# A gated linear unit on one core: the stores move from the ScalarE queue to the sync queue, behind the loads

## The chip, the core and the metric

The kernel runs on one core of one Trainium2 chip. The metric is the device time of one execution in microseconds (us). A difference of about 0.2% is what the measurement of this kernel can tell from no change.

## What is computed

The input `x` is 8192 x 8192 in float32. Its left half is `a`, its right half is `b`, and the result is 8192 x 4096:

```python
def reference(x):
    a, b = np.split(x, 2, axis=-1)
    return a * (1 / (1 + np.exp(-b)))
```

So 268.4 MB are read and 134.2 MB are written, and each output element needs one sigmoid and one product.

## The kernel before

**Tiles.** The rows are cut into 32 tiles of 256 rows. A tile has 128 partitions with two whole rows each, so a load is 128 x 16384 elements (64 KB in a partition, 8.39 MB in all) and a store is 128 x 8192 elements (32 KB in a partition, 4.19 MB). There are two slots (`SLOTS = 2`): two input tiles `x_sb0` and `x_sb1`, and two output tiles `o_sb0` and `o_sb1`. Tile i uses slot i modulo 2 of both.

**Work on a tile** (`work`, from L53). ScalarE takes the sigmoid of the `b` half in place (L61), and VectorE multiplies the `a` half by it into the output tile (L72). A middle tile is one piece: one activation and one product of 128 x 8192. The first and the last tile are cut into four pieces of 128 x 2048.

**Loads** (`load`, L46 to L51). All are issued on the sync queue, SP. Load i + 2 goes into the slot of tile i, so it waits until the products have counted up to the last one of tile i (`self.done[i]`, L50). Loads 0 and 1 wait for nothing; load 0 is moved ahead of the program's body.

**Stores** (`store`, L78 to L89). The store of a middle tile is issued on the ScalarE queue, ACT (L81, L82), and waits for the same count as load i + 2, the last product of tile i (L83). The last tile's store is cut into four pieces of 1 MB, one for each piece of the work, and these are issued on SP. When a store has landed it adds 16 to the slot's semaphore `ready` (L88). The first activation on a slot adds 1 to the same semaphore (L66), and the product waits for both together (L64, L65, L73): a product on tile i starts when its sigmoid is done and when store i - 2, which read the same output slot, has landed.

**Order** (`trace`, L91 to L104). It is written out by hand: load 1; then for each i the work of tile i, load i + 2 (if there is one) and store i (if i is not the last); then the four stores of the last tile. Each engine's sequencer goes through its own instructions in this order, and an instruction that waits holds up those behind it on the same engine. Before the change SP thus holds load 1, load 2, load 3 and so on and the four last stores, and ACT holds the activations of tile 0, store 0, the activation of tile 1, store 1 and so on. The data itself is moved by 16 DMA engines that serve both queues; q1 is the row of SP's transfers in the profile, q10 that of ACT's.

**End** (`close`). Each engine's drain, a wait for the last whole store, a clearing of the semaphores, and SP's wait for the four last stores (L118).

Of the kernel before, what the change touches and what calls it, by code (L numbers as in the profile page):

```python
# [1 line left out]

# [4 lines left out]

P = 128
R = 2
SLOTS = 2  # L10


class _Program:

    def __init__(self, nc, x, out):
        self.nc = nc
        fp32 = mybir.dt.float32
        n_rows, n_cols = x.shape
        self.half = n_cols // 2  # L30
        self.n_tiles = n_rows // (P * R)
        self.x = x.rearrange("(n p r) m -> n p (r m)", p=P, r=R)
        self.out = out.rearrange("(n p r) m -> n p (r m)", p=P, r=R)
        self.xs = [nc.alloc_sbuf_tensor(f"x_sb{s}", [P, R * n_cols], fp32).ap() for s in range(SLOTS)]
        self.os = [nc.alloc_sbuf_tensor(f"o_sb{s}", [P, R * self.half], fp32).ap() for s in range(SLOTS)]
        self.loaded = [nc.alloc_semaphore(f"loaded{s}") for s in range(SLOTS)]
        self.ready = [nc.alloc_semaphore(f"ready{s}") for s in range(SLOTS)]
        self.product = nc.alloc_semaphore("product")
        self.sigmoid = nc.alloc_semaphore("sigmoid")
        self.arrived = nc.alloc_semaphore("arrived")  # L40
        self.last = nc.alloc_semaphore("last")
        self.to_ready = [0] * SLOTS
        self.products = self.sigmoids = self.lasts = 0
        self.done = {}

    def load(self, i, after=None):  # L46
        s = i % SLOTS
        ins = self.nc.sync.dma_start(out=self.xs[s][:, :], in_=self.x[i]).then_inc(self.loaded[s], 16)
        if i >= SLOTS:
            ins._wait_ge(self.product, self.done[i - SLOTS])  # L50
        return ins  # L51

    def work(self, i, pieces):  # L53

        nc, s = self.nc, i % SLOTS
        rows = self.xs[s].rearrange("p (r h m) -> p r h m", r=R, h=2)
        packed = self.os[s].rearrange("p (r m) -> p r m", r=R)
        waits = []
        for k, (r, c) in enumerate(pieces):
            b = rows[:, r, 1, c]  # L60
            sig = nc.scalar.activation(out=b, in_=b, func=mybir.ActivationFunctionType.Sigmoid)  # L61
            if k == 0:
                sig._wait_ge(self.loaded[s], 16 * (i // SLOTS + 1))
                self.to_ready[s] += 1 + (16 if i >= SLOTS else 0)  # L64
                waits.append((self.ready[s], self.to_ready[s]))  # L65
                sig.then_inc(self.ready[s], 1)  # L66
            else:
                self.sigmoids += 1
                waits.append((self.sigmoid, self.sigmoids))
                sig.then_inc(self.sigmoid, 1)  # L70
        for (r, c), wait in zip(pieces, waits):
            mul = nc.vector.tensor_mul(out=packed[:, r, c], in0=rows[:, r, 0, c], in1=rows[:, r, 1, c])  # L72
            mul._wait_ge(*wait)  # L73
            mul.then_inc(self.product, 1)
            self.products += 1
        self.done[i] = self.products

    def store(self, i, lo=0, hi=None, products=None):  # L78
        s, final = i % SLOTS, i == self.n_tiles - 1
        hi = R * self.half if hi is None else hi  # L80
        queue = self.nc.sync if final else self.nc.scalar  # L81
        ins = queue.dma_start(out=self.out[i][:, lo:hi], in_=self.os[s][:, lo:hi])  # L82
        ins._wait_ge(self.product, self.done[i] if products is None else products)  # L83
        if final:
            self.lasts += 16
            ins.then_inc(self.last, 16)
        else:
            ins.then_inc(self.ready[s], 16)  # L88
        return ins  # L89

    def trace(self):  # L91

        n, half = self.n_tiles, self.half
        whole = [(slice(0, R), slice(0, half))]
        fourths = [(slice(r, r + 1), slice(h * half // 2, (h + 1) * half // 2)) for r in range(R) for h in range(2)]
        self.load(1)
        for i in range(n):
            self.work(i, fourths if i in (0, n - 1) else whole)
            if i + SLOTS < n:
                self.load(i + SLOTS)  # L100
            if i < n - 1:
                self.store(i)
        for k in range(4):
            self.store(n - 1, k * half // 2, (k + 1) * half // 2, self.products - 3 + k)  # L104

    def close(self):


        nc, s = self.nc, (self.n_tiles - 2) % SLOTS
        for engine in (nc.scalar, nc.vector, nc.sync):  # L110
            engine.drain().then_inc(self.arrived, 1)  # L111
        nc.gpsimd.wait_ge(self.arrived, 3)
        nc.gpsimd.wait_ge(self.ready[s], self.to_ready[s] + 16)
        ids = sorted(h.num for h in (*self.loaded, *self.ready, self.product, self.sigmoid, self.arrived))
        assert ids == list(range(ids[0], ids[-1] + 1)) and self.last.num not in ids
        nc.gpsimd.sem_clear(range(ids[0], ids[-1] + 1))
        nc.gpsimd.drain()
        nc.sync.wait_ge(self.last, self.lasts).then_inc(self.last, -self.lasts)  # L118


def _launch_early(nc):

    SP = mybir.EngineType.SP
    entry, body = (b.instructions for b in nc.main_func.blocks[:2])
    load = next(i for i in body if i.engine == SP and i.opcode == "DMACopy")
    assert not load.sync_info.on_wait
    body.remove(load)
    where = next(k for k, i in enumerate(entry) if i.engine == SP and i.opcode == "Drain")  # L130
    entry.insert(where, load)


@with_exitstack
def kernel(
    ctx: ExitStack,
    tc: tile.TileContext,
    x: bass.AP,
    out: bass.AP,
):  # L140
    nc = tc.nc
    prog = _Program(nc, x, out)
    tc.info.no_tile_sem_insts.add(prog.load(0).ins.name)
    tc.close()
    tc.compile()  # L145
    _launch_early(nc)
    prog.trace()
    prog.close()


# [1 line left out]
_INS = ['x']  # L152
_OUTS = [((8192, 4096), 'float32')]


# [23 lines left out]
```

## Time and profile before

| | |
|---|---|
| median of 3 runs | 933.18 us (933.16 to 934.11) |
| the profiled execution | 933.08 us |
| its span, from the first to the last instruction | 931.8 us |
| VectorE busy | 278.6 us (30% of the span), 38 products |
| ScalarE busy | 226.8 us (24%), 38 activations and a table load |
| moved by DMA | 402.67 MB, mean 432 GB/s over the span |
| one activation of 128 x 8192 | 7.03 us |
| one product of 128 x 8192 | 8.69 us |
| one activation, one product of 128 x 2048 | 1.90 us, 2.29 us |
| issue of a load on SP, of a store on ACT (median) | 0.33 us, 0.36 us |

The profile is of one execution, and its times run from the start of its span. "DMA share" in a stretch of time is the mean busy share of the 16 DMA engines, and GB/s is what they moved; both count a packet whole at its start, so a short stretch can show a share over 1. A "landing" is the moment at which all 16 parts of a transfer have reported to its semaphore. "Issue to landing" starts when the sequencer issues the transfer, so it holds the time that the transfer stands in its queue.

### The profile page before, as it was taken

Reading aid. Unit: us, or ns where it says so; the run is one execution under the profiler, and the core shown is the slowest. Engines: PE = TensorE matmul, PEld = TensorE weight load, DVE = VectorE, ACT = ScalarE, POOL = GpSimd, SP = SyncE. Lnnn points to the kernel's source line nnn. Section 1 sums busy time; section 2 is a strip of 40 time slices with the busy share of each in tenths; the row PEclk is TensorE's granted clock in tenths of the full one; section 3 lists DMA queues with packets and bytes.
Section 4 is the critical chain, followed back from the end, with each engine's and each line's share of the span. In section 5 each row is a group of like instructions: output and inputs, shape, how many; then the busy total and the mean of one; then the engine's idle time right before and its main releaser. Section 6 shows DMA issues by size and latency. Waiting matters only on the chain.

```text
span 931.8 us, 190 instructions
## 1 busy us (share of the span) xinstructions
DVE 278.6 (30%) x38; ACT 226.8 (24%) x39; POOL 0.2 (0%) x4
## 2 busy tenths in 40 slices
DVE  0333213333133331233312333123331233312333
ACT  1323330233311333113331133311333203332033
POOL 0000000000000000000000000000000000000000
DMA  9999999999999999999999999999999999999999
GB/s 405 428 450 428 422 456 405 450 428 428 450 421 435 428 436 442 428 428 450 450 405 430 442 456 428 412 463 408 450 428 428 450 408 447 428 428 450 426 429 405
DMA packets 9649, 402.67 MB, mean 432 GB/s; under 512 B 1072, under 2 KB 1072, under 8 KB 1072
## 3 DMA queue, kind: packets, MB, share of 16 engines
q1 hardware_dynamic: 5184, 272.63, 67.7%
q10 hardware_dynamic: 4464, 130.03, 32.3%
q14 instruction: 1, 0.01, 0.0%
HBM read 268.44 MB, written 134.22 MB: 432 GB/s over the span
## 4 chain that ended last, share of the span: by engine, by line
DMA 73%; DVE 15%; ACT 12%; DVEq 0%; issue 0%
DMA x_sb<-in_x_dram 73%; DVE o_sb L72 15%; ACT x_sb L61 12%; DVEq L111 0%
## 5 line engine op out<-in xcount | busy, mean ns | idle before, releaser
L72 DVE TENSOR_TENSOR o_sb<-x_sb 128x8192 f32<-128x8192 f32 (+1 forms) x38 | 278.6, 7344 | 647.1 <-ACT x_sb L61 647.1
L61 ACT ACTIVATE x_sb<-x_sb 128x8192 f32<-128x8192 f32 (+1 forms) x38 | 225.5, 5949 | 693.9 <-DMA x_sb<-in_x_dram 693.9
L61 ACT ACT_TABLE_LOAD x1 | 1.3, 1283 | 1.4 <-PEq L145 1.4
L163 POOL MEMSET const-bfloat16-1.0<- 128x1 bf16 x1 | 0.1, 102 | 0.0
L163 POOL MEMSET const-uint8-127<- 128x1 uint8 x1 | 0.1, 102 | 0.0
L163 POOL MEMSET const-float32-0.0<- 128x1 f32 x1 | 0.1, 99 | 0.2 <-issue 0.2
L163 POOL MEMSET const-float32-1.0<- 128x1 f32 x1 | 0.1, 99 | 0.0
## 6 DMA issues: line engine op xcount, KB each, us to landing
out_dram<-o_sb ACTq DMA_DIRECT2D x31, 4096.0 KB, 34.8
out_dram<-o_sb SPq DMA_DIRECT2D x4, 1024.0 KB, 5.7
x_sb<-in_x_dram SPq DMA_DIRECT2D x32, 42.2
```

The lines of the kernel that those rows point to most:

```text
L61: sig = nc.scalar.activation(out=b, in_=b, func=mybir.ActivationFunctionType.Sigmoid)
L72: mul = nc.vector.tensor_mul(out=packed[:, r, c], in0=rows[:, r, 0, c], in1=rows[:, r, 1, c])
L163: nc = _bacc.Bacc("TRN2", target_bir_lowering=False, num_devices=1)
```

## The change

The store's queue is no longer chosen: every store is issued on SP. Load i + 2 and store i keep their waits, both for the last product of tile i, and the written order is the same, so that SP now holds load 1, load 2, store 0, load 3, store 1, up to load 31, store 29, store 30 and the four last stores. Tiles, slots, pieces and semaphores stay as they are.

```diff
     def store(self, i, lo=0, hi=None, products=None):
         s, final = i % SLOTS, i == self.n_tiles - 1
         hi = R * self.half if hi is None else hi
-        queue = self.nc.sync if final else self.nc.scalar
-        ins = queue.dma_start(out=self.out[i][:, lo:hi], in_=self.os[s][:, lo:hi])
+        ins = self.nc.sync.dma_start(out=self.out[i][:, lo:hi], in_=self.os[s][:, lo:hi])
         ins._wait_ge(self.product, self.done[i] if products is None else products)
```

## The prediction

> **What bounds the kernel now.** I read the page first: the row of the DMA engines, the queues, and the chain that ended last.
>
> ```profile
> DMA  9999999999999999999999999999999999999999
> ...
> q1 hardware_dynamic: 5184, 272.63, 67.7%
> q10 hardware_dynamic: 4464, 130.03, 32.3%
> ...
> DMA 73%; DVE 15%; ACT 12%; DVEq 0%; issue 0%
> DMA x_sb<-in_x_dram 73%; DVE o_sb L72 15%; ACT x_sb L61 12%; DVEq L111 0%
> ```
>
> The chain of waits is misleading here. It goes load, sigmoid, product, load, and seems to say that VectorE and ScalarE carry 27% of the time. But the first line shows no slice in which the 16 DMA engines rest, and the two queues together took 67.7 + 32.3 = 100% of the engines' time. While the chain stands on a sigmoid or a product, the engines move the other slot's load and the store. So the bound is the DMA engines' throughput. The queue lines say one more thing: q1 moved 272.63 of 402.67 MB, which is 67.7%, and took 67.7% of the time. A byte loaded costs what a byte stored costs.
>
> Next the busy time by stretch, at places where different kinds of traffic are in flight. Columns: the stretch and its length, busy time of VectorE, ScalarE, GpSimd, TensorE's clock, DMA share, GB/s.
>
> ```profile
> 4.00:21.00 17.00, 0.00 (x0) 0.00 (x0) 0.00 (x0) 1.00 1.01 439
> 21.00:33.00 12.00, 8.90 (x4) 7.31 (x4) 0.00 (x0) 1.00 0.98 426
> 33.00:39.00 6.00, 0.00 (x0) 0.00 (x0) 0.00 (x0) 1.00 1.04 382
> ...
> 44.80:902.00 857.20, 260.77 (x30) 210.84 (x30) 0.00 (x0) 1.00 1.00 434
> 914.20:921.00 6.80, 4.24 (x2) 6.18 (x4) 0.00 (x0) 1.00 0.91 395
> 921.50:931.00 9.50, 4.16 (x2) 0.63 (x1) 0.00 (x0) 1.00 0.99 418
> ```
>
> Packets count at their start, so the rate of a busy engine is GB/s divided by the share. Loads alone on q1: 439/1.01 = 435, and 426/0.98 = 435 across the border of load 0 and load 1, which lies near 21. Loads and stores mixed over two queues: 434. Store 30 alone on q10: 395/0.91 = 434. The four 1 MB stores in a row on q1: 418/0.99 = 422, their packets being smaller. One stretch is out of line: 33 to 39, where 382/1.04 = 367. There the engines were "busy" 1.04 x 6 = 6.24 us for 382 x 6 = 2292 KB, which at 434 take 5.28 us: about 0.9 us were lost, just before the first store's packets. The trace's packet records agree: on all 16 engines the load packet ahead of store 0's first one took 3.2 to 3.5 us where 2.42 is the rule.
>
> Last, the chain in order of time (start, length, what), for the period:
>
> ```profile
> 60.54 42.07 DMA x_sb<-in_x_dram
> 102.61 0.02 issue
> 102.64 7.04 ACT x_sb L61
> 109.67 0.02 issue
> 109.70 8.70 DVE o_sb L72
> 118.40 0.02 issue
> 118.42 42.30 DMA x_sb<-in_x_dram
> ```
>
> Two tiles take 57.9 us here. From tile 1's sigmoid (44.76 in the timeline) to tile 31's (914.82) are 30 tiles in 870.06 us, 29.00 each. A tile's 12.58 MB at 434 GB/s are 29.0 us: the period is the transfer itself. By bytes, 19.33 us of it are the load and 9.67 the store.
>
> **The sum before.** 32 x 29.00 = 928.0. The last store at 422 instead of 434 adds 0.3. That is 928.3 of a span of 931.8; the rest, 3.5 us, is the start up to the first data, the 0.9 us, and the end after the last packet. The span's 931.8 and 1.3 us around it make the profiled execution's 933.08, which lies 0.1 below the median.
>
> **The change part by part.**
>
> *Issues.* 31 stores leave ACT (31 x 0.36 = 11 us) and go to SP (the four stores that SP issues now have a median of 0.34 us, so 31 x 0.34 = 10.5 us). ACT waits 693.9 us in all for loads, SP 860.9 us for products in front of the loads. A store is issued 0.33 us later than now, as load i + 2 precedes it with the same wait. Cost 0; the cover is the queue worked out below, some 20 us deep.
>
> *Waits.* None is new. Load i + 2 and store i await the same product, so neither holds the other up. Behind them on SP stand load i + 3 and store i + 1, which need a later product anyway. On ACT, the sigmoid of tile i + 1 no longer stands behind store i; this gains nothing, because product 1 ended at 60.5 and the load that the next sigmoid awaits landed at 73.6.
>
> *Order of the data.* This is what really changes. Now each engine alternates between a load's and a store's packets; afterwards q1 holds load 0, 1, 2, store 0, load 3, store 1, and so on, moved one after another. Call T the landing of load i. Store i - 2 is moved until T + 9.67, load i + 1 until T + 29.0, store i - 1 until T + 38.67. The sigmoid ends at T + 7.04; the product must await store i - 2 (its output slot), so it runs from T + 9.7 to about T + 18.5. Then load i + 2 and store i enter the queue, which has work until T + 38.67. So the queue never runs dry, with 20 us to spare, and the new wait of VectorE (2.6 us behind the store instead of the sigmoid) is covered by this.
>
> *End.* Load 31 lands 29 us before the last byte (about 901, now 914.8). Store 29 follows until +9.67 and store 30 until +19.33. The four last products of 2.29 us begin at +9.7; the first is done at +12, the last at about +18.9, so the first piece is there 7 us before it is needed, and each next one too. No gap; the end costs what it does now.
>
> *Borders in one queue.* There will be 59 changes of kind in q1: 30 from load to store, 29 from store to load. No row shows one, since now they fall between two queues. The bounds: from below nothing (a border may also save what the present one lost), from above the 0.9 us of the only costly border in the trace. The nearest rows are those without a gap: load 0 to load 1 in one queue, the four last stores in one queue, and about 16 changes of kind per tile between the queues, in a period that leaves no room for any cost. I take 0 for each. The 0.9 us I count as the first use of the second queue, since no later store pays it and the first load packet of q1 at the start was late by a similar 0.5 to 0.9 us (packet records). The second queue is gone, so I take these 0.9 us off.
>
> Sum: 933.08 - 0.9 = **932.2**. Not one byte fewer is moved, and no engine rests now, so nothing much is there to be gained or to be lost.
>
> A page speaks against 0 for a border. The Trainium skill, "DMA: Bandwidth & Descriptors", section on the anatomy of one DMA, gives a transfer a fixed cost of about 2.0 us, mostly the wait for the receipt of its last write. If one queue showed this cost at each of the 59 borders, the estimate by that page would be 118 us more, 1050 us. The trace bears it out only where nothing else is queued: the four 1 MB stores at the end pass within 9.7 us, which is their bytes.
>
> **The rivals.**
>
> *A change of kind drains the engine (slower).* Mechanism: in one queue the first store packet reads SBUF only when the load's last write to it is through, and the 0.9 us at 36 was that, not the first use of a queue; afterwards two queues hid it by having the other's packets ready. For it: exactly that border was the costly one, on every engine. Against: the borders without a gap above. Price: at loads to stores alone 30 x 0.9 = 27, 959 us (10 in 100); at both kinds of border 59 x 0.9 = 53, 985 us (4 in 100); a part of it, up to 0.5 us at 30 borders, 935 to 947 us (11 in 100). It decides from 0.06 us a border (1.9 us in all, the 0.2%).
>
> *The queue takes no more (slower).* Up to four transfers stand in q1 at once, against two loads now. If SP blocks until one is through, load i + 2 still has 20 us; only if not even one can stand behind the one in flight does the queue run dry. Then each of 62 transfers pays a start like the first one's 0.7 us: 43 us, 975 us. Two loads stand in it now, which speaks against it (3 in 100).
>
> *The engines like long runs (faster).* With fewer changes between packets, the rate might rise from 434. The rows with loads alone give 435, and at 435 all would take 926 + 3.5 + 1.3 - 0.9, or 930: faster by 0.3% (5 in 100).
>
> *The change does not do what it says.* That the order on SP delays something that now goes early is excluded by the equal waits; a store is in fact delayed, from 34.8 us between issue and landing to about 49, and the only one to wait for it is the product, as worked out.
>
> **How the numbers follow.** A difference of 0.2%, 1.9 us, is about what a measurement of this kernel can tell from no change. Forecast, 931.3 to 935: 67 in 100. Rivals as given, 14 + 11 + 3 slower, 5 faster. The range goes down to 929.5, about where no overhead but the ends is left, and up to 947, half a drain per border. It leaves out 17 in 100 above. Within 0.2%: 0.67; slower 0.28; faster 0.05.
>
> **What would show it.** In the profile after: q10 gone and q1 at 100%; the DMA row still all nines; 434 GB/s in the middle; load 1 landing near 41 instead of 44.7, load 2 near 60.5 instead of 73.6; issue to landing about 39.5 us for a load (now 42.2) and 49 for a store (now 34.8); VectorE released by a store's landing instead of ScalarE; and 33 to 39 at 434. Wrong would be a period over 29.0 at a DMA share of 1 (drains), or a share under 1 (the queue ran dry).

## The result, and the profile after

The changed kernel takes 938.00 us (median of 4 runs, 937.89 to 938.72), the kernel before 933.19: ratio 1.005, 95% interval 1.0037 to 1.0062. It is slower by 4.8 us, 0.5%. The profiled executions took 937.89 and 933.08 us, with spans of 936.3 and 931.8.

The page of the changed kernel, DMA row, queue, chain, and issues (from issue to landing, median):

```profile
DMA  9999999999999999999999999999999999999998
...
q1 hardware_dynamic: 9648, 402.66, 99.7%
...
DMA out_dram<-o_sb 73%; DVE o_sb L72 16%; DMA x_sb<-in_x_dram 4%; ACT x_sb L61 1%; SPq L48 0%; DVEq L110 0%
...
out_dram<-o_sb SPq DMA_DIRECT2D x31, 4096.0 KB, 49.1
...
x_sb<-in_x_dram SPq DMA_DIRECT2D x32, 39.7
```

Much came as forecast: the second queue is gone, a store takes 49.1 us from issue to landing and a load 39.7, and the chain now goes over the stores, since a product waits for its output slot. The DMA engines never rest in the middle. What is new is small and stands at the right end of the first row: the last slice is an 8.

The timeline of ScalarE and VectorE (start, length) shows the landings, as the sigmoid starts at the landing of its load:

```profile
41.13 7.03 ACT L61 ACTIVATE x_sb<-x_sb 128x8192 f32<-128x8192 f32 x1 [12.02 <-DMA x_sb<-in_x_dram]
61.59 7.03 ACT L61 ACTIVATE x_sb<-x_sb 128x8192 f32<-128x8192 f32 x1 [13.43 <-DMA x_sb<-in_x_dram]
71.44 8.69 DVE L72 TENSOR_TENSOR o_sb<-x_sb 128x8192 f32<-128x8192 f32 x1 [14.55 <-DMA out_dram<-o_sb]
90.69 7.03 ACT L61 ACTIVATE x_sb<-x_sb 128x8192 f32<-128x8192 f32 x1 [22.07 <-DMA x_sb<-in_x_dram]
...
907.12 7.31 ACT L61 ACTIVATE x_sb<-x_sb 128x2048 f32<-128x2048 f32 x4 [22.00 <-DMA x_sb<-in_x_dram]
```

Load 1 landed at 41.1 as forecast, load 2 at 61.6 instead of 60.5, and load 31 at 907.1 instead of 901. From 90.69 to 907.12 are 28 tiles, 29.16 us each instead of 29.00.

Now busy time by stretch, changed kernel (the two columns at the end are the DMA share and GB/s):

```profile
33.00:39.00 6.00, 0.00 (x0) 0.00 (x0) 0.00 (x0) 1.00 1.21 524
55.00:61.00 6.00, 1.88 (x1) 0.00 (x0) 0.00 (x0) 1.00 0.97 350
44.80:902.00 857.20, 260.76 (x30) 207.20 (x30) 0.00 (x0) 1.00 1.00 433
930.00:931.50 1.50, 0.00 (x0) 0.00 (x0) 0.00 (x0) 1.00 0.80 339
931.50:933.00 1.50, 0.00 (x0) 0.00 (x0) 0.00 (x0) 1.00 0.26 109
933.00:934.50 1.50, 0.00 (x0) 0.00 (x0) 0.00 (x0) 1.00 0.19 82
```

and the last three stretches for the kernel before:

```profile
930.00:931.50 1.50, 0.00 (x0) 0.00 (x0) 0.00 (x0) 1.00 0.57 240
931.50:933.00 1.50, 0.00 (x0) 0.00 (x0) 0.00 (x0) 1.00 0.00 0
933.00:934.50 1.50, 0.00 (x0) 0.00 (x0) 0.00 (x0) 1.00 0.00 0
```

Two things are to be seen. The 0.9 us that were lost between 33 and 39 have moved, not gone: 33 to 39 is now at 524/1.21 = 433, but 55 to 61, where the first store follows load 2, is at 350/0.97 = 361, that is 0.97 x 6 - 350 x 6 / 434 = 1.0 us lost. And before, all 16 engines are done by 931.5; in the changed kernel a share of 0.26 is still busy then, which is 4 engines of 16.

The trace's packet records, taken apart engine by engine, agree. (A record doesn't name its engine; a packet is put on the engine whose last packet ended just as it starts.) In the kernel before, the engines end between 930.7 and 931.4 us. In the changed one, twelve end between 930.9 and 931.6, and four at 933.8, 934.1, 935.3 and 935.9. These four did not rest: some of their packets took longer. It is nearly always the same packet, the last one of a load when a store comes next in the queue. I call a packet late when the next starts more than 15 ns later than usual. At the first border from a load to a store all 16 engines were late, by 15.4 us in all; at the later ones 75 packets were, by 16.7 us in all, of which the four last engines have 13.8. Borders from a store to a load, and from a load to a load, show next to none. By time, the 16.7 us are 1.4 (80 to 145), 7.9 (145 to 290), 4.7, 2.2, 0.5 in stretches of 145 us, and nothing after 725. The largest single delay after the first border is 0.73 us, at the first one 1.25. So the time went to few engines, in the first half, and was never given back, as each engine has its own eight packets of every transfer. The engine that ended last was late by 4.2 us at borders after the first one and by 0.3 us in other packets; it ended at 935.9, the last engine of the kernel before at 931.4, and these 4.5 us are the difference of the spans.

### The profile page after: what moved, and what is told of

The parts are those of the page before. It is cut to its first block, busy times and chain, and to the rows that moved or that the text cites. A ratio compares the mean times of both kernels' runs of the same rounds, so it can differ in the third digit from the quotient of the medians.

```text
span 936.3 us, 190 instructions
## 1 busy us (share of the span) xinstructions
DVE 278.6 (30%) x38; ACT 226.8 (24%) x39; POOL 0.2 (0%) x4
## 4 chain that ended last, share of the span: by engine, by line
DMA 77%; DVE 16%; another core or an unknown queue 4%; ACT 1%; SPq 0%; DVEq 0%; issue 0%
DMA out_dram<-o_sb 73%; DVE o_sb L72 16%; DMA x_sb<-in_x_dram 4%; ACT x_sb L61 1%; SPq L48 0%; DVEq L110 0%
## 5 line engine op out<-in xcount | busy, mean ns | idle before, releaser
L72 DVE TENSOR_TENSOR o_sb<-x_sb 128x8192 f32<-128x8192 f32 (+1 forms) x38 | 278.6, 7344 | 647.2 <-DMA out_dram<-o_sb 607.9
## 6 DMA issues: line engine op xcount, KB each, us to landing
out_dram<-o_sb SPq DMA_DIRECT2D x31, 4096.0 KB, 49.1
x_sb<-in_x_dram SPq DMA_DIRECT2D x32, 39.7
```

## The experiments

**The theories.** A: every border from a load to a store in one queue has a price, on the last engine 4.8 us / 30 = 0.16 us. B: engines are late as long as they cross the border together; what falls behind is spared, so the loss ends when a few engines are some 5 us behind. C: VectorE and ScalarE, working on SBUF, get in the way. D: it is new output memory. W and R: it is the turn of the engine's writes, or of its reads.

The packet records of all runs, read as above (us of late packets in all 16 engines after the first border, and the first and the last engine to end; the ratio is to runs of the kernel before that were taken along with each):

| run | median, ratio to before and interval | late packets | engines end |
|---|---|---|---|
| before | 933.19 | 1, 0.2 us | 930.7 to 931.4 |
| changed | 938.00, 1.005 (1.0037 to 1.0062) | 75, 16.7 us | 930.9 to 935.9 |
| e1_swap | 933.87, 1.0001 (0.9992 to 1.0010) | 1, 0.3 us | 930.8 to 931.4 |
| e2_first8 | 936.80, 1.0039 (1.0024 to 1.0054) | 91, 18.5 us | 934.1 to 935.2 |
| e3_last16 | 937.80, 1.0049 (1.0032 to 1.0066) | 150, 38.1 us | 932.4 to 935.3 |
| e4_small_work | 938.80, 1.0067 (1.0043 to 1.0091) | 98, 21.5 us | 931.1 to 937.0 |
| e5_store_first | 938.36, 1.0049 (1.0034 to 1.0064) | 89, 23.6 us | 932.9 to 936.9 |
| e6_halves | 938.76, 1.0054 (1.0037 to 1.0071) | 103, 21.2 us | 934.2 to 937.6 |
| e7_same_out | 938.54, 1.0055 (1.0040 to 1.0070) | 91, 17.9 us | 932.8 to 938.8 |
| e14_lag_in_queue | 937.84, 1.0044 (1.0027 to 1.0061) | 12, 2.0 us | 930.9 to 935.8 |

The first engine's end is not always a measure of its own delays: in e2 load 31 landed at 919.0 us instead of 914.8, so the last stores were issued late, and the engines that were ahead stood idle (a share of 0.57 between 920 and 925 us). In e7, the profiled execution was the slowest of four (940.6 us; the others 937.4 to 939.3).

**Is it the one queue, or the issuer?** Loads on ACT, stores on SP:

```diff
-        ins = self.nc.sync.dma_start(out=self.xs[s][:, :], in_=self.x[i])...
+        queue = self.nc.sync if i < SLOTS else self.nc.scalar
+        ins = queue.dma_start(out=self.xs[s][:, :], in_=self.x[i])...
...
-        queue = self.nc.sync if final else self.nc.scalar
+        queue = self.nc.sync
```

> Loads from tile 2 on are issued on ACT, all stores on SP: two queues again, with the issuers exchanged. If the cost comes from loads and stores sharing one queue (theories A and B below), the time is that of before, 933.2 us, and no load's last packet is late at a later store. If it comes from issuing the stores on SP instead of ACT, the time is that of the change, 938.0.

The time is that of before, with one late packet. Stretches of this run:

```profile
44.80:902.00 857.20, 260.78 (x30) 210.87 (x30) 0.00 (x0) 1.00 1.00 434
930.00:931.50 1.50, 0.00 (x0) 0.00 (x0) 0.00 (x0) 1.00 0.61 257
931.50:933.00 1.50, 0.00 (x0) 0.00 (x0) 0.00 (x0) 1.00 0.00 0
```

All engines end together. That stores are issued on SP costs nothing; that loads share the queue with them does.

**A price per border, or a bounded loss?** Only the first eight stores, only the last ones, and twice as many borders:

```diff
-        queue = self.nc.sync if final else self.nc.scalar
+        queue = self.nc.sync if final or i < 8 else self.nc.scalar
```

> Stores 0 to 7 go on SP behind the loads, stores 8 to 30 on ACT as before: 8 of the 30 borders from a load to a store in one queue. Theory A (every such border costs the same on the engine that ends last: 4.8 us / 30 = 0.16 us): 933.2 + 8 x 0.16 = 934.5 us. Theory B (a border costs only while the 16 DMA engines cross it close together; each delay sets an engine back, and once some engines are 3 to 5 us behind no more is lost): the slowest engine was 3 us behind after 8 borders of the changed kernel by its packet records, and the lag should stay in the two-queue part: 936.2 us.

Measured: 936.8, where A gives 934.5 and B 936.2. Eight borders of thirty make 3.6 of the 4.8 us (0.39% of 0.5%).

```diff
-        queue = self.nc.sync if final else self.nc.scalar
+        queue = self.nc.sync if i >= 14 else self.nc.scalar
```

> Stores 14 to 30 go on SP behind the loads, stores 0 to 13 on ACT as before: some 16 borders, late in the kernel. Theory A: 933.2 + 16 x 0.16 = 935.8 us. Theory B: the engines come to the first such border as close together as at the start, so 16 fresh borders set the slowest back by what the first 16 did, 4.5 us: 937.7 us. If only the start of the kernel were costly (something that is cold), the time would be 933.2 to 933.6, since the last 16 borders of the changed kernel cost 0.4 us.

Measured: 937.8; B gave 937.7, A 935.8 (ratio 1.0028, just below the interval). In this run, the first load with a store behind it in the same queue ends at 467 us. Stretches up to the end of that store and from there on:

```profile
44.80:478.00 433.20, 130.83 (x16) 112.47 (x16) 0.00 (x0) 1.00 1.00 434
478.00:902.00 424.00, 129.93 (x15) 98.41 (x14) 0.00 (x0) 1.00 1.00 432
```

The engines are undisturbed for 478 us and lose afterwards. Theory B did not foresee everything here: all 16 engines crossed the border at 467 us within 0.5 us of each other and none was late, while at the next one all 16 were; and 38.1 us were lost in all, more than twice the changed kernel's 16.7. The last three borders, from 842 us on, had no late packet. So the changed kernel's second half is not cheap because it comes late, but because something has settled by then.

```diff
...
+        w = 2 * self.half
+        for c in (slice(0, R * w),) if after is None else (slice(after * w, (after + 1) * w),):
+            ins = self.nc.sync.dma_start(out=self.xs[s][:, c], in_=self.x[i][:, c]).then_inc(self.loaded[s], 16)
...
+            for r in range(R):
+                if i + SLOTS < n:
+                    self.load(i + SLOTS, r)
+                if i < n - 1:
+                    self.store(i, r * half, (r + 1) * half)
```

> The changed kernel with each load from tile 2 on and each middle store cut into two by row, in the order half load, half store, half load, half store: 60 borders from a load to a store instead of 30. The smaller packets alone add about 2.5 us by the packet records (64 KB 2.414 us, 32 KB 1.2095, 8 KB 0.306, so about 5 ns more for each added packet). Theory A: 933.2 + 2.5 + 60 x 0.16 = 945.3 us. Theory B (the lag is bounded at some 5 us): 933.2 + 2.5 + 4.8 = 940.5 us, or less if shorter runs settle sooner.

Measured: 938.8, against 945.3 by A and 940.5 or less by B. Of the 21.2 us that packets were late after the first border, 14.7 fell before 100 us: with twice the borders it settled sooner. Theory A falls with these three runs.

**Is it the order, the computing, or the memory written?**

```diff
+            if i < n - 1:
+                self.store(i)
             if i + SLOTS < n:
                 self.load(i + SLOTS)
-            if i < n - 1:
-                self.store(i)
```

> The changed kernel with store i issued ahead of load i + 2, so that q1 holds load 0, load 1, store 0, load 2, store 1, load 3 and so on: one queue, 31 borders from a load to a store, but each store is moved 29 us earlier. Theories A and B (the border in one queue is what costs): as the change, 936.5 to 938.5 us. If the cost lay in this order's late stores (products waiting for the output slot), the time would be that of before, 933.2.

```diff
-        whole = [(slice(0, R), slice(0, half))]
+        whole = [(slice(0, R), slice(0, 256))]
...
+        for o in self.os:
+            self.nc.vector.memset(o, 0.0)
+        self.nc.vector.drain()
```

> The changed kernel with the same loads and stores, but sigmoid and product on 256 of the 4096 columns of each row only (128 of 2048 in a piece of the first and last tile); the rest of the output tiles is filled with zeros once at the start. Theory C (VectorE and ScalarE, working on SBUF, get in the way of the DMA engines at the border): the loss goes, 933.2 to 934 us. Theories A and B: the loss stays, 937 to 938.5 us.

```diff
-        ins = self.nc.sync.dma_start(out=self.out[i][:, lo:hi], in_=self.os[s][:, lo:hi])
+        ins = self.nc.sync.dma_start(out=self.out[i if final else s][:, lo:hi], in_=self.os[s][:, lo:hi])
```

> The changed kernel, but all stores except those of the last tile write to the first two tiles of the output in turn (the rest of the output is left unwritten). Theory D (the delay at the border is the first touch of output memory that was not written before): only the first two borders cost, 933.5 us or less. Theories A and B: as the change, 937 to 938.5 us.

All three stay slow: 938.4, 938.8 and 938.5. The stores' place behind the loads, the work on SBUF (theory C) and the first touch of output memory (theory D) are out. In e7, 55 of the 91 late packets fell after 290 us, the last ones at 907 us: there the loss had not died out by the end, and the last engine came to the last border 7.7 us behind the first, so 5 us is not a bound in every execution.

**What turns at the border?** Both are made from e4, where the control is:

```diff
-        ins = self.nc.sync.dma_start(out=self.out[i][:, lo:hi], in_=self.os[s][:, lo:hi])
+        src = self.os[s][:, lo:hi] if final else self.x[i][:, lo:hi]
+        ins = self.nc.sync.dma_start(out=self.out[i][:, lo:hi], in_=src)
```

> As the run with little work on VectorE and ScalarE (one queue, load i + 2 ahead of store i), but the middle stores read the same number of bytes from the input in HBM instead of the output tile in SBUF: a copy from HBM to HBM (so the output is not the reference's). The border then changes only where the DMA engine writes, not where it reads. Theory W (the delay at the border comes with the turn of the writes, from SBUF to HBM): packets ahead of the copy are still late at many borders, some 30 us in all over the 16 engines as in the run it is made from. Theory R (it comes with the turn of the reads, from HBM to SBUF: the read of the store cannot start early): none are late, and the engines end within 1 us of each other. The copy itself may run at another rate, so the time is no measure.

```diff
+        h = self.half
+        dst = self.out[i][:, lo:hi] if final else self.os[s][:, h:2 * h]
+        src = self.os[s][:, lo:hi] if final else self.os[s][:, 0:h]
+        ins = self.nc.sync.dma_start(out=dst, in_=src)
```

> As the run with little work, but the middle stores write half an output tile into its other half: a copy from SBUF to SBUF of half the bytes, 16 KB packets (so the output is not the reference's and only the last tile is stored). The border then changes only where the DMA engine reads, not where it writes. Theory R: packets ahead of the copy are still late at many borders. Theory W: none are late. With 134 MB less to HBM and 65 MB of copies in its place the time is near 268 + 65 + 4 = 337 MB at 434 GB/s, 777 us, plus 4 us at the ends; it is no measure of the border.

Neither theory alone holds. In e9 only 2 of some 480 last load packets were late, by 0.06 us together, and not even the first border cost anything; but the copies themselves were slow (a 32 KB packet 1.33 us in the median instead of 1.21; 1001 us in all), so its silence counts for less. Its engines also drifted apart without any border's help, by 3.3 us at the fourth border and some 7 us by the end, where theory B expects no loss anyway, so only its first few borders say anything. In e10, 786 us, all 16 engines were late at the first border, by 17.4 us in all, and none ever after. A copy that turns only the reads is spared. As it also moved half the bytes, I ran the control, the same half tile in the same packets, but to HBM:

```diff
...
+        dst = self.out[i][:, lo:hi] if final else self.out[i][:, h:2 * h]
+        src = self.os[s][:, lo:hi] if final else self.os[s][:, 0:h]
...
```

> The control for the copy from SBUF to SBUF: the run with little work, but each middle store writes only half of its tile to HBM, in the same 16 KB packets from the same place as that copy (so half of the output is not written). If the copy had no late packets because it does not turn the writes to HBM, this run has them: over 8 us in all 16 engines after the first border. If it had none because of its size, this run has none either: under 1 us. The time, from 268 + 65 + 4 = 337 MB at 434 GB/s, is near 781 us plus what is lost.

787.2 us, and 61 packets were late after the first border, by 13.3 us; the last engine ended at 785.3, in e10 at 784.2. So the later losses need a store that writes to HBM, and the size is not it. They seem to need the turn of the reads as well (e9), which is less sure.

**Does a lag spare an engine?** Four engines were to be set behind at the start, by four small loads on ACT:

```diff
+        for o in self.os:
+            for p in (0, 32):
+                self.nc.scalar.dma_start(out=o[p:p + 4, :], in_=self.x[0][p:p + 4, 0:R * half]).then_inc(self.warm, 16)
+        self.nc.vector.wait_ge(self.warm, 64)
```

> The changed kernel with four small extra loads on the ACT queue at the very start, each of 4 partitions x 32 KB (they are overwritten by the first products); each should run on four DMA engines only, one packet of 1.21 us each, and set those four 4.8 us behind the other twelve before the first border. If the losses at the borders come on top of any lag (theory A), the time is 938.0 + 4.8 = 942.8 us. If a lag of about 5 us is where the losses end (theory B), the four engines lose little more and the others stay within what they lost in the changed kernel: 938 to 939 us, with the last engines ending where they did in the changed kernel.

A miss by both: 953.2 us, ratio 1.0212 (1.0195 to 1.0229). The stretches show where it went:

```profile
0.00:10.00 10.00, 0.00 (x0) 1.28 (x1) 0.20 (x4) 1.00 1.11 321
10.00:30.00 20.00, 0.00 (x0) 0.00 (x0) 0.00 (x0) 1.00 0.98 295
30.00:45.00 15.00, 1.40 (x1) 3.34 (x2) 0.00 (x0) 1.00 1.00 350
```

By the share the rate is 289 and 301 GB/s instead of 434: while the small loads ran, the packets of the loads took mostly up to 2.9 us longer too (one 3.5), 11.5 us on the mean engine before 45 us, and the small packets themselves took 3 to 4.7 us (the last one 1.6) instead of 1.21. Why, no run shows. Load 0 landed at 41.7 instead of 21.8. So its time says nothing on A or B. Its later packets do: some 25 late ones, 2.1 us, instead of 75 and 16.7. Because that is a by-product of a run that missed its aim, I put the lag into the one queue, as small copies between loads 1 and 2:

```diff
         self.load(1)
+        for p in (0, 32, 64, 96):
+            self.nc.sync.dma_start(out=self.out[n - 1][p:p + 4, :], in_=self.x[0][p:p + 4, 0:R * half]).then_inc(self.warm, 16)
```

> The changed kernel with four small copies from HBM to HBM on SP between load 1 and load 2, each of 4 partitions x 32 KB into rows that the last tile's stores write again. If they run on four DMA engines only, these are 5 to 6 us behind the others from 47 us on, before the first border. If a lag spares an engine (theory B), the losses after the first border are below 5 us over the 16 engines, and the time is 933.2 + 5 to 6 = 938 to 940 us. If losses come on top of any lag (theory A): 938 + 5 to 6, 943 to 944 us. If the small copies hold up all 16 engines as the small loads at the start did, the time says nothing and the packet records after 80 us decide.

937.84 us, ratio 1.0044 (1.0027 to 1.0061): the changed kernel's own time, though four engines had 4.9 us more to do (sixteen packets of 1.21 us, four on each of four engines, by the records). The stretches of this run:

```profile
80.00:902.00 822.00, 247.76 (x29) 196.81 (x28) 0.00 (x0) 1.00 1.00 434
...
930.00:931.50 1.50, 0.00 (x0) 0.00 (x0) 0.00 (x0) 1.00 0.75 317
931.50:933.00 1.50, 0.00 (x0) 0.00 (x0) 0.00 (x0) 1.00 0.34 142
933.00:934.50 1.50, 0.00 (x0) 0.00 (x0) 0.00 (x0) 1.00 0.27 115
934.50:936.00 1.50, 0.00 (x0) 0.00 (x0) 0.00 (x0) 1.00 0.19 82
```

434 after the first border, where the changed kernel had 433, and four engines that end late (a share of 0.27), by about the lag they were given. After the first border 12 packets were late, 2.0 us in all, 1.75 of it on one engine. By theory A this run would be 943. Of the twelve others, the one with the 1.75 us fell back to 2.5 us behind the first; the other eleven go on crossing their borders within 0.6 us of each other and are late once, by 0.03 us, as the twelve leading engines of the changed kernel are late only three times after 200 us, by 0.13 us together. So it is not enough for a delay that engines cross together, as theory B had it; with four engines out of the way nearly all others pass. That a lag spares engines holds here; that it is crossing together which costs does not, and the size of the bound is not fixed (e7).

**The 0.9 us ahead of the first store.** Two attempts on the kernel before: a tiny store on SP between loads 0 and 1, and a tiny load on ACT at the start:

```diff
+        self.nc.gpsimd.memset(self.tiny, 0.0).then_inc(self.warm, 1)
+        first = self.nc.sync.dma_start(out=self.out[n - 1][:, 0:128], in_=self.tiny)
...
```

> The kernel before, with a tiny store (512 B a partition, into columns that the last tile's store writes again) on SP between load 0 and load 1; the other stores stay on ACT. The question is the 0.9 us that all 16 engines lost ahead of store 0. If they belong to the first use of the second queue, they stay at 33 to 39 us: 933.3 us. If they belong to the first store of the program, they are paid at the tiny store instead or go: 932.3 to 933.3 us, and 33 to 39 us shows 434 GB/s by the share.

```diff
+        self.nc.scalar.dma_start(out=self.tiny, in_=self.x[0][:, 0:128]).then_inc(self.warm, 16)
```

> The kernel before, with a tiny load (512 B a partition, into a tile that nobody uses) on the ACT queue at the very start, so that the second queue has been used before store 0. If the 0.9 us ahead of store 0 are the first use of that queue, they go, and the time is 932.3 us. If they belong to the first turn from loads to a whole store (as in the changed kernel, which never uses the second queue and lost them as well), they stay: 933.3 us, and 33 to 39 us still shows about 365 GB/s by the share.

Both stay: 933.5 us (ratio 1.0001, 0.9991 to 1.0010) and 934.3 (1.0005, 0.9996 to 1.0015). First e8, then e11:

```profile
33.00:39.00 6.00, 0.00 (x0) 0.00 (x0) 0.00 (x0) 1.00 0.97 350
```

```profile
33.00:39.00 6.00, 0.09 (x1) 0.00 (x0) 0.00 (x0) 1.00 0.96 350
```

361 and 365 GB/s by the share, where 434 is the rule. So it is neither the first use of the second queue nor the first store of any size. It was there at the first whole transfer that reads SBUF in each run whose packets I took apart, the copy within SBUF too, and not in e9, where nothing but the last tile reads SBUF. Nor does it belong to the border of an engine: in e14 the four engines that were behind lost 0.75 to 0.92 us at the same moment as the others, 57 us, in the middle of a load. So it is a loss of its own, paid once.

## Why the prediction was wrong, point by point

The forecast was 932.2 us, no change; measured are 938.0. Of the 5.8 us between, 0.9 were taken off and did not go, 4.5 are the later end of the last engine, and the rest, 0.4, lies outside the span and in the choice of the execution.

*The bound* was right: the DMA engines, at 434 GB/s, with no rest. *Issues and waits* cost nothing, as worked out: e1 issues all stores on SP and takes 933.9, and VectorE's new wait for stores (607.9 us in all in the changed kernel) delays nothing. *The order of the data* was right in each landing up to the first border, and the queue never ran dry; the rival of a full queue is out.

*Borders in one queue* is the step that failed: "I take 0 for each". I had taken rows without a gap as the nearest, but each of them lacked something: load 0 to load 1 and the four last stores have no change of kind, and the many changes of kind in the kernel before lie between two queues. The term measures 4.2 us on the engine that ends last. The one costly row, 0.9 us at the only border from loads to a store, was no measure of it either: e10 and e14 show that it is a one-time loss, and at all 30 borders it would have given 959 us. So no row before the change had this term, and nothing but the bounds, 0 to 0.9 us a border, was known of it.

*The 0.9 us* is the second term that failed, by its explanation: I took it off as the first use of the second queue. It stayed, 1.0 us at 55 to 61, in a kernel without that queue, and e11 shows that using the queue earlier doesn't help.

*The end* failed with the first: "the end costs what it does now" holds only if the engines arrive together. A transfer is done when the last of its 16 parts is, so load 31 landed at 907.1 instead of 901 though twelve engines had their parts by 902 or so.

*The rivals.* The drain at a change of kind was the right family, and its partial form (11 in 100) had the time, 935 to 947; but it was thought of as a price at 30 borders, and e2, e3 and e6 show that it is not. That the measured time lies in its range, and in the whole range given (929.5 to 947), is luck. The two full drains (959 and 985 us) are out. The page cited against 0, the Trainium skill's "DMA: Bandwidth & Descriptors", with 2.0 us a transfer, describes in that section transfers issued from GpSimd; here they are issued from SP and ACT. At borders its cost is not borne out: 4.2 us over 30 borders on the last engine are 0.14 each. Where nothing stood ahead in the queue, load 0 took 21.8 us from issue to landing, 2.5 us more than its bytes at 434 GB/s. The same page's section "Issuing engines are not separate DMA queues" states that starting DMAs from several engines saves only issue time. By that rule the change would have cost nothing, as issue time is hidden here; that was the forecast's own result. The runs differ, 938.0 against 933.2 us and back to 933.9 with two queues in e1, and the measurement decides.

*What stays open:* which unit holds the last load packet back, why eleven or twelve engines pass a border together where sixteen mostly do not (in e3 all 16 passed one), and why the engines that fall behind first are the ones that go on falling. In e7 the last three of them were still late near the end. The runs show the condition (one queue, a store from SBUF to HBM behind a load), and that the loss dies out in the changed kernel when four engines are 3 to 5 us behind; they do not show the mechanism, nor a fixed bound. None of the versions beats the kernel before.

## What to carry to other kernels

Where a kernel is bound by the DMA engines, loads and stores on two queues can be worth having even though the same engines carry both: in this kernel 0.5%, with issue time and waits fully hidden. Busy engines at the full rate don't say that they end together, so read the last slices by the share (0.26 is four engines of sixteen) before believing that a queue order is free. And a term for which the trace has no row of the same kind is not 0 because rows of other kinds show no gap: no row here had a store waiting behind a load in one queue, and a run with a few stores moved, like e2, measures the term.

## What the runs showed of the hardware that was not expected

- In one queue, a load's last packet is often late when a store to HBM comes next: up to 0.73 us, in 75 packets of the changed kernel after the first border (up to 1.25 us in e4 and e7), until four engines were 3 to 5 us behind (in e7 it went on to 7.7); with four engines set 4.9 us behind beforehand, 2.0 us in all instead of 16.7.
- The first whole transfer out of SBUF costs each engine about 0.9 us, whichever queue carries it (0.8 to 1.1 in the kernel before, 0.6 to 1.3 in the changed one). In e14 the four engines that were behind lost 0.75 to 0.92 us at the same moment, 57 us, in the middle of their load: it hit all engines at once, not each at its own border.
- Four small loads on four engines, on the second queue at the start, slowed all sixteen: 289 to 301 GB/s by the share instead of 434, and load 0 landed 20 us later. The same amount in one queue behind load 1 (e14), there as copies from HBM to HBM, held up only its own four.
- A copy from HBM to HBM took 1.33 us for a 32 KB packet (median, e9), a store 1.21.
